# Attention's scores by pairs of heads, in the two halves of TensorE's rows

## The chip, the cores and the metric

The kernel runs on one core of a Trainium2 chip. The time is that of the device, in microseconds, for one execution of the whole program: the median of several runs, and one more execution that the hardware profiler recorded. Engines are called as in the profile: PE is TensorE (matmul; PEld its weight loads), DVE is VectorE, ACT is ScalarE, POOL is GpSimd and SP issues the large DMAs.

## What is computed

The reference is an encoder of two layers on 512 tokens of width 1024, in float32. Each layer mixes tokens in three parallel groups, then applies experts and a gated embedding:

```python
for i in range(DEPTH):                       # 2 layers
    xn = rmsnorm(x, g_mix[i])
    proj = xn @ w_in[i]                      # split into the inputs of the groups
    y_a = gmlp_spatial_gating(...)           # 4 groups x 64
    y_b = dilated_attention(b_q, b_k, b_v, positions, ...)   # 6 heads x 64
    y_c = gated_deltanet(...)                # 6 heads x 64, forward and backward scans
    x = x + concat(y_a, y_b, y_c) @ w_out[i]
    x = x + expert_choice_ffn(rmsnorm(x), ...)               # 16 experts
    x = x + rmsnorm(p[i] @ w_ple[i]) * sigmoid(rmsnorm(x) @ w_ple_gate[i])
```

In `dilated_attention` q and k are normed per head and partly rotated. Three patterns of window and dilation are mixed by their softmax denominators. That equals one softmax over all 512 keys with a mask that holds the logarithm of how many patterns allow a key (and -1e30 where none does), which is how the kernel computes it.

## The kernel before

`mixer` (L363) does the three groups of a layer. It first projects and prepares them; then the scan of the gated delta net, `gdn_scan` (L907), runs as the leading work, and three other pieces of work fill the time in which it waits: attention's v projection (`attn_v`, L595), attention itself (`core`, L608) and the first part of the output projection (`w_out_first`, L1015), one after the other. All four are generators that yield a number after each piece.

`interleave` (L446) sets the order. It runs three pieces of the fill, then again and again one piece of the scan and as many pieces of the fill as the scan's piece asked for: the number that a scan piece yields (`FILLS`, 1.9, 1.5 and 1.1) is added to what is owed, the number that a fill piece yields is its price and is taken off, and the next scan piece comes once 0.5 or less is owed. PE follows the pieces in just this order, since each is issued after the last PE instruction of the piece before (`in_order`, L427). Instructions on the other engines are ordered by a planner that estimates times, each engine working off its own queue in order. What is left of the fill when the scan has ended follows it (L421), then the rest of the delta net (`gdn_out`, L985, which norms and gates the scan's sum and transposes it), and the second part of the output projection (`w_out_last`, L1034).

A step of the scan treats one chunk of 32 tokens in both directions; there are 16. Its pieces on PE are pK (L929), pV (L943), pS (L958) and pO (L969). Between them DVE makes tm (L932) and rr (L936) from pK, ACT copies pV to vn (L947), DVE adds pS to the state St (L962) and adds up the outputs (L977, L979), in the later half with POOL (L980). Each step waits for the state of the last.

In attention a q tile holds two heads, one in partitions 0 to 63 and the other in 64 to 127. `attn_qk` (L464) keeps each q tile twice, with zeros in the other head's half (L473 to L475), so that a matmul over all 128 rows with the k tile of both heads gives the scores of one head. `core` goes over units of one head, one tile of 128 queries: `first` makes the scores (128 x 512) in one PSUM bank out of two, and lets DVE add the mask and take the maximum (L621), ACT take the exponential (L624) and DVE divide by the sum (L626); `second`, two units later, transposes the result by PE (L632) and copies it by ACT (L634); `third`, for each pair of heads, multiplies by v (L641), and `split` stores the result in two parts. The prices are 0.9 for `first`, 0.5 for `second` and 0.9 for `third`. Each float32 matmul shows in the profile as two records, a transpose as one.

Weights of the projections are split into a high and a low half as they come in (`wnext`, L311), by ACT (L330) and POOL (L332, wlo); they lie in slots that are shared with other tensors, and a split can start once such a slot is free.

Of the kernel before, what the change touches and what calls it, by code (L numbers as in the profile page):

```python
# [11 lines left out]
F32 = mybir.dt.float32  # L12
F32R = mybir.dt.float32r
I32 = mybir.dt.int32
AF = mybir.ActivationFunctionType
# [6 lines left out]
S = 512  # L22
DEPTH = 2
NT = S // 128
# [9 lines left out]
THETA = 500000.0  # L34
C_AU, C_BQ, C_CQ, C_GATE, C_A = 0, 512, 1664, 2816, 3200
SLOTS = 12

OWED = 0.5

# [70 lines left out]
class K:  # L110
# [252 lines left out]
    def mixer(self, l):  # L363
        nc, tc, A = self.nc, self.tc, self.A
        with tc.tile_pool(name=f"mix{l}", bufs=1, reuse_waits="tile") as mp:
            self.mp = self.sm = mp
            self.t = lambda i, shape, name: mp.tile(shape, F32, tag=f"t{i}", name=name, bufs=2)
            self.p1 = lambda shape, name: mp.tile(shape, F32, tag="p1", name=name, bufs=3)
            self.p2 = lambda shape, name: mp.tile(shape, F32, tag="p2", name=name, bufs=2)
            self.one = lambda shape, name: mp.tile(shape, F32, tag=name, name=name, bufs=1)  # L370

            for tag, n, bufs in (("qk", 1024, 2), ("amask", S + 384, 1), ("wsT", 512, 1), ("mcst", CROUTE - CKEEP, 1),
                                 ("p1", 512, 3), ("p2", 512, 2)):
                for _ in range(bufs):
                    mp.tile([128, n], F32, tag=tag, name="place", bufs=bufs)
            self.mark("norm")
            g = self.gslot("grow")[:, :D]
            self.row(g, l, "g_mix")
            win, wo = A["w_in"][l], A["w_out"][l]
            specs = [(win[:, c:c + n], n, KD) for c, n in  # L380
                     [(C_AU, 256), (C_AU + 256, 256)]]
            specs += [(win[512 * i:512 * i + 512, C_GATE:C_GATE + 408], 408, 4) for i in range(2)]
            specs += [(win[:, c:c + n], n, KD) for c, n in
                     [(C_CQ + 128 * b[0], 128 * len(b)) for b in QKV_BLOCKS]
                     + [(C_BQ + 256 * i, 256) for i in range(3)]]
            specs += [(win[512 * i:512 * i + 512, C_BQ + 768:C_BQ + 1152], 384, 4) for i in range(2)]
            specs += [(wo[0:640, c:c + n], n, 5) for c, n in WO_COLS]
            specs += [(wo[640:1024, 512 * i:512 * i + 512], 512, 3) for i in range(2)]
            self.wplan(specs)
            wuv = [self.wnext()]  # L390
            if l == 0:
                self.load_x(range(1, NT))
            xs = self.gslot("xs").rearrange("p (t d) -> p t d", t=2)
            tv = lambda name: self.slot(name).rearrange("p (k n) -> p k n", k=4)
            self.xh, self.xl = [tv("xh") for _ in range(2)], [tv("xl") for _ in range(2)]
            for t in range(NT):
                if t == 2:
                    wuv.append(self.wnext(pieces=4))
                self.norm(t, g, xs[:, t % 2, :])
                self.norm_T(t, xs[:, t % 2, :], self.xh, self.xl)  # L400
            self.setup2(l)
            self.gmlp(l, wuv)
            self.gate_decay(l)

            qkv = self.gdn_qkv(l)
            next(qkv)
            self.gdn_chunk(l)
            wq = self.wnext(ahead=False)
            next(qkv, None)
            self.gdn_inv(l)  # L410
            self.gmlp_out(l)
            if l == 0:
                self.trig()
            nc.scalar.dma_start(self.amask, A["amask"])
            self.attn_qk(l, wq)
            self.gdn_inv_T(l)
            wv = [self.wnext(small=True), self.wnext()]

            other = chain(self.attn_v(l, wv), self.core(l), self.w_out_first(l))
            self.interleave(self.gdn_scan(l), other)  # L420
            for _ in other:  # L421
                pass
            self.wo2 = [self.wnext() for _ in range(2)]
            self.gdn_out(l)
        self.w_out_last(l)
# [38 lines left out]
    def attn_qk(self, l, wq):  # L464
        self.mark("attn_qk")
        nc, mp = self.nc, self.mp
        v, act, pe, pool_e = nc.vector, nc.scalar, nc.tensor, nc.gpsimd

        at = [self.slot("att") for _ in range(3)]
        qT = self.qT = [a[:, 0:2 * S].rearrange("p (e n) -> p e n", e=2) for a in at]  # L470
        kT = self.kT = [a[:, 2 * S:3 * S] for a in at]
        self.vat = [a[:, 3 * S:].rearrange("p (t n) -> p t n", t=NT) for a in at]
        for q in qT:  # L473
            pool_e.memset(q[64:128, 0, :], 0.0)
            pool_e.memset(q[0:64, 1, :], 0.0)  # L475

        g2 = self.small([128, 2, 64], "g2")
        o = PR["q_g"][0]
# [6 lines left out]
        gT = self.small([128, 2], "gT")  # L485
# [6 lines left out]
        def second(i, t, qk):  # L492

            pt = self.pc([128, 2, 128], "qkTp")
            for j in range(2):
                pe.transpose(pt[:, j, :], qk[:, t, 2 * j:2 * j + 2, :].rearrange("p h d -> p (h d)"), self.ident)
            ts = slice(t * 128, (t + 1) * 128)
            for j in range(2):
                b = 2 * i + j
                if b < 3:  # L500
                    act.activation(qT[b][0:64, 0, ts], pt[0:64, j], AF.Copy, scale=gT[0:64, 0:1])
                    act.activation(qT[b][64:128, 1, ts], pt[64:128, j], AF.Copy, scale=gT[64:128, 0:1])
                else:
                    act.activation(kT[b - 3][:, ts], pt[:, j], AF.Copy, scale=gT[:, 1:2])

# [100 lines left out]
                self.nc.scalar.activation(self.vat[j][:, t, :], p[:, 128 * j:128 * j + 128], AF.Copy)  # L606

    def core(self, l):  # L608
        nc = self.nc
        v, act, pe = nc.vector, nc.scalar, nc.tensor  # L610
        yb = [self.slot("yTb")[:, :3 * S].rearrange("p (j n) -> p j n", j=3) for _ in range(2)]
        self.yTb = yb
        PTs = {}

        def first(j, t, hp):
            p = self.pb([128, S], "sc")
            pe.matmul(p, self.qT[j][:, hp, t * 128:(t + 1) * 128], self.kT[j], start=True, stop=True)
            P = self.p1([128, S], "P")
            mx = self.small([128, 1], "mx", 3)
            sm_ = self.small([128, 1], "smx", 3)  # L620
            v.tensor_tensor_reduce(P, p, self.amask[:, 384 - 128 * t:384 - 128 * t + S], scale=1.0,  # L621
                                   scalar=-3e38, op0=ALU.add, op1=ALU.max, accum_out=mx)
            v.tensor_scalar(mx, mx, -1.0, None, op0=ALU.mult)
# [19 lines left out]
            ts = slice(t * 128, (t + 1) * 128)  # L643
            self.split(yb[0][:, j, ts], yb[1][:, j, ts], po)

        units = [(j, t, hp) for j in range(3) for t in range(NT) for hp in range(2)]
        Ps = {}
        for i in range(len(units) + 3):
            self.mark("core")
            if i < len(units):  # L650
                Ps[i] = first(*units[i])
                yield 0.9
            if 0 <= i - 2 < len(units):
                self.mark("core")
                second(*units[i - 2], Ps.pop(i - 2))
                yield 0.5
            if i - 3 >= 0 and units[i - 3][2]:
                self.mark("core")
                third(*units[i - 3][:2])
                yield 0.9  # L660


    def gate_decay(self, l):
# [833 lines left out]
```

## Time and profile before

| | |
|---|---|
| median of three runs | 1959.53 us (1959.13 to 1962.07) |
| the profiled execution | 1958.17 us, span 1956.2 us |
| PE busy | 1799.0 us, 92% of the span |
| DVE busy | 930.7 us, 48% |
| ACT busy | 523.6 us, 27% |
| POOL busy | 457.6 us, 23% |
| attention's core in layer 0, first scores to last product with v | 255.87 to 353.00 us |
| the same in layer 1 | 1222.00 to 1319.00 us |

The profiled execution took 1958.17 us as a whole; times in the trace count from the start of its span. Busy times of the engines overlap, so their shares don't add up to one. Matmuls are pipelined: the shown duration of one reaches into the next, and what a row of equal matmuls costs is better read from one start to the next.

### The profile page before, as it was taken

To read this page: it belongs to the slowest core of one execution; us is meant where nothing else is said; L and a number is where in the kernel's file an instruction comes from. 1 tells how busy PE (TensorE), PEld (TensorE's weight loads), DVE (VectorE), ACT (ScalarE), POOL (GpSimd) and SP (SyncE) were. 2 spreads that over 40 slices of the span, in tenths; PEclk is the share of its full clock that TensorE was granted. 3 is DMA by queue.
4 is the path that set the end of the run, shared out by engine and by line. 5 is a ranking of instruction groups with operands and counts; after the bars stand their busy time and mean duration, and the time that the engine had idled before them with its cause. 6 is when DMAs were issued, how large, how long until landed. Compare 5 with 4: busy or idle time off the path is not lost.

```text
span 1956.2 us, 30065 instructions
## 1 busy us (share of the span) xinstructions
PE 1799.0 (92%) x12216; PEld 1126.8 (58%) x12216; DVE 930.7 (48%) x2088; ACT 523.6 (27%) x1213; POOL 457.6 (23%) x402
## 2 busy tenths in 40 slices
PE   5898698979999999999988978899799999999998
PEld 5777665864434444335987767568544343443368
DVE  5879868661211111422788896786511212114135
ACT  4334444231111101102443344452211010011032
POOL 3544413420000003201645352233100000022033
PEclk9989889989999999999998978899799999999999
DMA  5212020287899999999242020204798999999981
GB/s 169 87 34 60 17 85 16 109 321 296 347 412 412 390 412 411 366 414 374 85 131 82 21 71 24 76 2 168 305 356 345 412 406 395 415 372 393 414 289 65
DMA packets 168730, 467.46 MB, mean 239 GB/s; under 512 B 11664, under 2 KB 68496, under 8 KB 168592
## 3 DMA queue, kind: packets, MB, share of 16 engines
q1 hardware_dynamic: 161504, 458.46, 61.0%
q10 hardware_dynamic: 7088, 7.09, 1.2%
q8 instruction: 96, 1.57, 0.3%
q14 instruction: 42, 0.34, 0.1%
HBM read 461.32 MB, written 4.19 MB: 238 GB/s over the span
## 4 chain that ended last, share of the span: by engine, by line
PE 68%; DVE 21%; ACT 4%; issue 3%; POOL 2%; DMA 2%; SPq 1%; ACTq 0%; DVEq 0%; POOLq 0%
PE pGt L1270 15%; PE pUp L1270 11%; PE pY L1270 10%; DVE acc L770 3%; PE xep L1198 2%; DVE rr L936 2%; PE ysc L1289 2%; PE xep L1199 2%; PE op L340 1%; PE ysc L1290 1%; PE pV L943 1%; PE plep L1164 1%; PE pgp L342 1%; PE pgp L340 1%; PE pY L1385 1%
## 5 line engine op out<-in xcount | busy, mean ns | idle before, releaser
L1270 PE MATMUL pUp<-w,xe 128*64 128x512 f32 x800 | 200.8, 595 | 0.0
L1270 PE MATMUL pGt<-w,xe 128*64 128x512 f32 x640 | 200.4, 600 | 0.0
L332 POOL TENSOR_TENSOR wlo<-w,whi 128x512 fp32r<-128x512 f32 (+5 forms) x66 | 161.3, 2463 | 114.7 <-ACT whi L330 99.9
L1270 PE MATMUL pY<-w,hidT 128*64 128x512 f32 x720 | 186.9, 596 | 0.0
L1337 POOL TENSOR_TENSOR x<-x,hh 128x1024 f32<-128x1024 f32 x8 | 18.9, 2358 | 615.5 <-DVE x L1295 615.4
L1270 PEld LDWEIGHTS pUp<-w,xe 128*64 128x64 f32 x800 | 70.7, 137 | 101.8 <-issue 98.0
L1295 DVE TENSOR_TENSOR x<-ysc,x 128x512 f32<-128x512 f32 x96 | 63.2, 686 | 117.9 <-PE ysc L1290 117.9
L1270 PEld LDWEIGHTS pGt<-w,xe 128*64 128x64 f32 x640 | 58.6, 136 | 99.7 <-issue 97.6
L1270 PEld LDWEIGHTS pY<-w,hidT 128*64 128x64 f32 x720 | 64.1, 136 | 89.9 <-issue 87.4
L1270 PE MATMUL pGt<-wx,xe 128*64 128x512 f32 x320 | 114.4, 603 | 0.3
L1328 DVE SCALAR_TENSOR_TENSOR hid<-sg,gsl,pUp 128x512 f32<-128x512 f32 x32 | 23.7, 747 | 159.7 <-PE pUp L1270 158.1
L1354 DVE SCALAR_TENSOR_TENSOR yl<-pY,gsl,yh 128x512 fp32r<-128x512 f32 x28 | 21.0, 751 | 165.2 <-ACT yh L1353 163.7
L1321 DVE SCALAR_TENSOR_TENSOR sg<-sg,pGt 128x512 f32<-128x512 f32 x32 | 21.8, 686 | 132.2 <-ACT sg L1320 132.2
L330 ACT ACTIVATE whi<-w 128x512 fp32r<-128x512 f32 (+5 forms) x66 | 68.0, 1058 | 38.5 <-PE op L341 15.8
L342 PE MATMUL pgp<-whi,gTl 128*128 128x256 f32 x256 | 72.8, 292 | 3.9 <-DVE gTl L271 3.9
L329 POOL TENSOR_TENSOR w<-w,pp 128x512 f32<-128x512 f32 x32 | 32.4, 1047 | 179.2 <-DMA w<-in_w_ple_gate_dram 107.7
L1320 ACT ACTIVATE sg<-pGt,gsl 128x512 f32<-128x512 f32 x32 | 21.8, 687 | 192.2 <-PE pGt L1270 190.2
L340 PE MATMUL pgp<-whi,gTh 128*128 128x256 f32 x256 | 73.0, 289 | 0.0
L1200 ACT ACTIVATE xe<-xep,pp 128x256 f32<-128x256 f32 x64 | 30.2, 474 | 158.7 <-PE xep L1199 158.7
L341 PE MATMUL pgp<-wlo,gTh 128*128 128x256 f32 x256 | 72.4, 288 | 0.0
L1198 PE MATMUL xep<-OH,hh 128*128 128x256 f32 x256 | 69.1, 304 | 2.5 <-DVE OH L1186 2.5
L1344 ACT ACTIVATE hidT<-htp 128x512 f32<-128x512 f32 x32 | 19.1, 597 | 193.5 <-PE htp L1343 193.5
(404 smaller groups left out, 4277.0 us busy)
## 6 DMA issues: line engine op xcount, KB each, us to landing
w<-in_w_e_up_dram SPq DMA_DIRECT2D x100, 1024.0 KB, 14.6
w<-in_w_e_down_dram SPq DMA_DIRECT2D x90, 1024.0 KB, 11.3
w<-in_w_e_gate_dram SPq DMA_DIRECT2D x80, 1024.0 KB, 12.9
wx<-in_w_e_gate_dram SPq DMA_DIRECT2D x40, 1024.0 KB, 11.6
wx<-in_w_e_up_dram SPq DMA_DIRECT2D x28, 1024.0 KB, 12.2
wx<-in_w_e_down_dram SPq DMA_DIRECT2D x22, 1024.0 KB, 8.3
wd<-in_w_e_down_dram SPq DMA_DIRECT2D x32, 512.0 KB, 8.8
w<-in_w_in_dram SPq DMA_DIRECT2D x14, 1024.0 KB, 5.0
```

The lines of the kernel that those rows point to most:

```text
L330: self.nc.scalar.activation(rr_(hi[:, ks, :]), wk, AF.Copy)
L332: e.tensor_tensor(rr_(lo[:, ks, :]), wk, hi[:, ks, :], op=ALU.subtract)
L340: pe.matmul(p, lh, rh, start=first, stop=False)
L341: pe.matmul(p, lh, rl, start=False, stop=False)
L342: pe.matmul(p, ll, rh, start=False, stop=last)
L770: v.scalar_tensor_tensor(acc, raw[:, kk:kk + S], conv[:, b, kk:kk + 1], acc, op0=ALU.mult, op1=ALU.add)
L936: v.tensor_tensor(rr[kl[dr], :], vtok[kl[dr], tl, :], fl(tm[kl[dr]]), op=ALU.subtract)
L1198: pe.matmul(p, rr_(hh[:, t, ks]), OHf[:, t, :], start=(t == 0), stop=False)
L1199: pe.matmul(p, rr_(hl[:, t, ks]), OHf[:, t, :], start=False, stop=(t == NT - 1))
L1270: pe.matmul(pt[nh][64 * ei:64 * ei + 64, :], lhs[:, kk, 64 * ei:64 * ei + 64], wt[ei][k][:, nh * 512:nh * 512 + 512], start=(kk == 0), sto ...
L1289: pe.matmul(p, rr_(OT[:, t, :]), rr_(yh[:, ns]), start=True, stop=False)
L1295: v.tensor_tensor(xv, p, xv, op=ALU.add)
```

## The change

The zeros and the second copy of q go. q and k tiles now hold two heads each in the two halves of the partitions, and a pair of heads is one unit. Its scores are four matmuls over 64 rows, in turns for the upper and the lower half of the array's rows, each for half of the keys; the two heads write to the two PSUM banks. The softmax of both heads follows. The order within a step of `core` becomes scores of unit i, product with v of unit i - 2, transposes of unit i - 1; the prices are 1.1, 0.9 and twice 0.5. The p1 buffers, which hold the exponentials, become four, and the DMA scratch is set to 256.

```diff
+P1 = 4
...
-            self.p1 = lambda shape, name: mp.tile(shape, F32, tag="p1", name=name, bufs=3)
+            self.p1 = lambda shape, name: mp.tile(shape, F32, tag="p1", name=name, bufs=P1)
...
-        qT = self.qT = [a[:, 0:2 * S].rearrange("p (e n) -> p e n", e=2) for a in at]
-        kT = self.kT = [a[:, 2 * S:3 * S] for a in at]
-        self.vat = [a[:, 3 * S:].rearrange("p (t n) -> p t n", t=NT) for a in at]
-        for q in qT:
-            pool_e.memset(q[64:128, 0, :], 0.0)
-            pool_e.memset(q[0:64, 1, :], 0.0)
+        qT = self.qT = [a[:, 0:S] for a in at]
+        kT = self.kT = [a[:, S:2 * S] for a in at]
+        self.vat = [a[:, 2 * S:3 * S].rearrange("p (t n) -> p t n", t=NT) for a in at]
...
-                    act.activation(qT[b][0:64, 0, ts], pt[0:64, j], AF.Copy, scale=gT[0:64, 0:1])
-                    act.activation(qT[b][64:128, 1, ts], pt[64:128, j], AF.Copy, scale=gT[64:128, 0:1])
+                    act.activation(qT[b][:, ts], pt[:, j], AF.Copy, scale=gT[:, 0:1])
...
-        def first(j, t, hp):
-            p = self.pb([128, S], "sc")
-            pe.matmul(p, self.qT[j][:, hp, t * 128:(t + 1) * 128], self.kT[j], start=True, stop=True)
-            P = self.p1([128, S], "P")
-            mx = self.small([128, 1], "mx", 3)
-            sm_ = self.small([128, 1], "smx", 3)
+        def first(j, t):
+
+            ps = [self.pb([128, S], "sc") for _ in range(2)]
+            for half in range(2):
+                cs = slice(half * S // 2, (half + 1) * S // 2)
+                for hp, p in enumerate(ps):
+                    hl = slice(64 * hp, 64 * hp + 64)
+                    pe.matmul(p[:, cs], self.qT[j][hl, t * 128:(t + 1) * 128], self.kT[j][hl, cs], start=True, stop=True)
+            return [softmax(p, t) for p in ps]
+
+        def softmax(p, t):
+            P = mp.tile([128, S], F32, tag="p1", name="P", bufs=P1)
+            mx = self.small([128, 1], "mx", 4)
+            sm_ = self.small([128, 1], "smx", 4)
...
-        units = [(j, t, hp) for j in range(3) for t in range(NT) for hp in range(2)]
+        units = [(j, t) for j in range(3) for t in range(NT)]
         Ps = {}
-        for i in range(len(units) + 3):
+        for i in range(len(units) + 2):
             self.mark("core")
             if i < len(units):
                 Ps[i] = first(*units[i])
+                yield 1.1
+            if 0 <= i - 2:
+                self.mark("core")
+                third(*units[i - 2])
                 yield 0.9
-            if 0 <= i - 2 < len(units):
-                self.mark("core")
-                second(*units[i - 2], Ps.pop(i - 2))
-                yield 0.5
-            if i - 3 >= 0 and units[i - 3][2]:
-                self.mark("core")
-                third(*units[i - 3][:2])
-                yield 0.9
+            if 0 <= i - 1 < len(units):
+                for hp in range(2):
+                    self.mark("core")
+                    second(*units[i - 1], hp, Ps[i - 1][hp])
+                    yield 0.5
...
-    nc = bacc.Bacc("TRN2", target_bir_lowering=False, num_devices=1)
+    nc = bacc.Bacc("TRN2", target_bir_lowering=False, num_devices=1, dynamic_dma_scratch_size=256)
```

## Rows read from the trace of the kernel before

**Rows 1.** The page, the chain that ended last: shares of the span by engine

```profile
PE 68%; DVE 21%; ACT 4%; issue 3%; POOL 2%; DMA 2%; SPq 1%; ACTq 0%; DVEq 0%; POOLq 0%
```

**Rows 2.** Windows by stage: length, busy us of PE, PEld, DVE, ACT, POOL, then PEclk, DMA

```profile
255.87:353.00 97.13, 85.47 (x1275) 57.74 (x1273) 75.39 (x210) 48.50 (x106) 27.46 (x22) 0.91 0.11 41
375.50:392.50 17.00, 15.40 (x109) 15.13 (x105) 13.45 (x33) 3.41 (x5) 5.87 (x5) 1.00 0.67 263
392.50:416.00 23.50, 23.18 (x129) 19.17 (x128) 15.16 (x51) 7.83 (x16) 0.80 (x2) 1.00 0.68 245
1222.00:1319.00 97.00, 85.31 (x1278) 57.60 (x1273) 75.27 (x210) 48.50 (x106) 27.43 (x22) 0.91 0.12 42
```

**Rows 3.** Windows by scan step: three undisturbed steps, one of three heads, two stalled

```profile
307.12:332.20 25.08, 23.78 (x396) 16.29 (x395) 20.14 (x64) 13.73 (x31) 6.41 (x7) 1.00 0.01 2
260.30:269.68 9.38, 8.61 (x131) 5.62 (x131) 7.83 (x26) 6.21 (x13) 0.50 (x2) 1.00 0.39 139
269.68:285.32 15.64, 12.06 (x130) 8.48 (x129) 10.34 (x23) 4.58 (x10) 5.42 (x3) 0.67 0.00 1
293.10:307.12 14.02, 10.07 (x130) 6.74 (x129) 10.90 (x23) 4.42 (x11) 4.79 (x2) 0.76 0.16 48
```

**Rows 4.** Timeline of PE, from a scan step: start, us, what (xcount are records)

```profile
321.89 0.86 PE L969 MATMUL pO<-vn,QKm 32*32 32x64 f32 x24
322.68 1.12 PE L617 MATMUL sc<-att 128*128 128x512 f32 x2
323.74 0.58 PE L929 MATMUL pK<-St,KQT 64*64 64x64 f32 x24
324.25 0.66 PE L632 MATMUL ptp<-cst,P 128*128 128x128 f32 x4
324.74 1.02 PE L617 MATMUL sc<-att 128*128 128x512 f32 x2
```

**Rows 5.** Timeline of PE in the experts: two column halves

```profile
485.33 0.59 PE L1270 MATMUL pY<-w,hidT 128*64 128x512 f32 x1
485.34 0.59 PE L1270 MATMUL pY<-wx,hidT 128*64 128x512 f32 x1
```

**Rows 6.** Groups of DVE in 307.12:332.20: count, then busy us and mean ns

```profile
L621 DVE CUSTOM_DVE_ANT_0 P<-sc,amask 128x512 f32<-128x512 f32 x7 | 4.7, 686 | 1.3 <-PE sc L617 1.3
L626 DVE TENSOR_SCALAR P<-P,smx 128x512 f32<-128x512 f32 x7 | 3.7, 522 | 0.1
L625 DVE RECIPROCAL smx<-smx 128x1 f32<-128x1 f32 x7 | 1.1, 162 | 2.9 <-ACT P L624 2.8
```

**Rows 7.** Timeline of POOL: a weight's low half

```profile
270.38 4.24 POOL L332 TENSOR_TENSOR wlo<-w,whi 128x1920 fp32r<-128x1920 f32 x1 [0.35 <-ACT whi L330]
```

**Rows 8.** Timeline of DVE: the scan's subtraction; a w_out addition and two steps of gdn_out

```profile
271.74 3.87 DVE L936 TENSOR_TENSOR rr<-vtok,tm 32x384 f32<-32x384 f32 x2
...
383.63 0.56 DVE L1031 TENSOR_TENSOR x<-op,x 128x384 f32<-128x384 f32 x1 [0.43 <-PE op L342]
...
385.76 2.88 DVE L182 SCALAR_TENSOR_TENSOR ro__4169<-nr,ro__4169 128x24 f32<-128x24 f32 x1
...
389.12 0.18 DVE L182 SCALAR_TENSOR_TENSOR ro__4169<-nr,ro__4169 128x24 f32<-128x24 f32 x1
```

**Rows 9.** Timeline of PE: after the stall; last scan matmuls; first transposes of gdn_out

```profile
275.18 1.97 PE L943 MATMUL pV<-rr,XT 32*32 32x64 f32 x24 [3.48 <-DVE rr L936]
...
374.71 0.86 PE L969 MATMUL pO<-vn,QKm 32*32 32x64 f32 x24
...
392.54 0.93 PE L1010 MATMUL ycp<-cst,o_sum 128*128 128x128 f32 x6
```

**Rows 10.** Windows: the stretches of lower clock behind the two stalls

```profile
275.10:285.30 10.20, 10.02 (x98) 7.35 (x98) 5.00 (x14) 2.54 (x6) 0.83 (x1) 0.51 0.01 2
300.50:305.00 4.50, 4.49 (x36) 2.81 (x38) 1.69 (x7) 2.14 (x5) 0.00 (x0) 0.50 0.50 149
```

**Rows 11.** Timeline of POOL: the first of the six memsets of q's padding

```profile
174.99 0.52 POOL L474 MEMSET att<- 64x512 f32 x1
```

More of the change, by code (lines that the diff above doesn't have):

```diff
@@ L372, in mixer @@
             for tag, n, bufs in (("qk", 1024, 2), ("amask", S + 384, 1), ("wsT", 512, 1), ("mcst", CROUTE - CKEEP, 1),
-                                 ("p1", 512, 3), ("p2", 512, 2)):
+                                 ("p1", 512, P1), ("p2", 512, 2)):
                 for _ in range(bufs):
@@ L608, in core @@
     def core(self, l):
-        nc = self.nc
+        nc, mp = self.nc, self.mp
         v, act, pe = nc.vector, nc.scalar, nc.tensor
```

## The prediction

> **What bounds the kernel now.** I read the page's chain first [rows 1]: 68% of the end is TensorE (PE), 21% VectorE (DVE). The change touches one stage of each layer, so I then cut the span into windows by stage [rows 2]. Attention's core runs beside the delta-net scan for 97.1 us in layer 0 and 97.0 us in layer 1, with the same busy times in both, so one layer is worked out and doubled. PE is busy 85.5 of the 97.1, but at a granted clock of 0.91; DVE 75.4. Steps of the scan [rows 3] show why: three undisturbed ones take 25.08 us (8.36 each) with PE busy 23.78, so PE is the bound and DVE, 20.14, is close behind. Two steps are far longer, 15.64 and 14.02. In the first, POOL works on a weight's low half for 4.24 us [rows 7], DVE's two rr subtractions take 3.87 [rows 8], and pV starts after 3.48 us of idle PE [rows 9]; behind each such wait PE runs at 0.50 to 0.51, half its 2.4 GHz, for 10.2 and 4.5 us [rows 10]. The two steps together lie 12.9 us over two of 8.36.
>
> What sets the scan's pace is a price list, not a time: a whole scan step releases 1.9 + 1.5 + 1.1 = 4.5 units of fill. The 97.1 us held 44.4 units of core, so 9.87 steps, and without the 12.9 a step took (97.13 - 12.94) / 9.87 = 8.53 us.
>
> **The scores.** One piece of scores (two records) starts 1.06 us before the next when it follows a scan piece; after transposes its 1.02 ends within the next piece, by some 0.1 as neighbours do, so about 0.9 [rows 4]. Mean 0.98, a pair of heads 1.96. Afterwards a pair is eight records of half the columns, and each half of the array's rows streams what one head streamed. If the halves run side by side the pair costs 0.98, if not 1.96. The nearest row is of column halves: two records of the experts start 0.01 us apart and both take 0.59 [rows 5]; and pK, 24 records over row and column halves, passes in 0.51 [rows 4]. I take 0.98: 12 pairs x 0.98 = 11.8 us less PE work a layer.
>
> The Trainium skill says otherwise on one point: its page "TensorEngine Tiling (Array Packing)", section "Key Properties", states that changing the tiling mode drains the engine. The pieces of rows 4 differ by 0.1 to 0.2 us after a change of shape, so the rule shows here; charged once more to each pair it would turn the sum below from -1.6 to +0.8 us a layer, which is the third rival.
>
> **Where the saving appears.** By the prices a pair falls from 2 x 0.9 + 2 x 0.5 + 0.9 = 3.7 units to 1.1 + 0.9 + 1.0 = 3.0; twelve pairs give 8.4 units less. The scan's own pieces are unchanged, so its steps keep asking for 4.5 units, and w_out's first part moves up by 8.4 units. In the scan's part PE therefore loses 11.8 us and gets 8.4 units of w_out: the fill's prices add up to 16 for v, 44.4 for core and 25.7 for w_out, 86.1, of which the three first pieces and the scan's 16 steps (2.6 + 15 x 4.5) spend 73.1; the other 13.0 made the tail with 15.4 us of PE [rows 2], 1.18 each, so 8.4 are 9.9 us. The scan ends about 1.9 us earlier, not 11.8. This needs core steps of 8.3 us (eight of them are left, and eight times 8.53 - 8.3 is 1.8, which I use).
>
> Does DVE allow 8.3? It has 20.14 / 3 = 6.7 us a step with 7/3 heads [rows 3, 6]. A step will hold 1.5 pairs, three heads. A head is 0.69 and 0.52 for the two large operations and about 0.3 for two small ones [rows 6], 1.5; so 6.7 + 0.67 x 1.5 = 7.7 us, 93% of 8.3. The one step of before with three heads had DVE 7.83 and took 9.38, but PE was busy 8.61 of that [rows 3]; taking away 1.5 pairs x 0.98 leaves 7.9. So a core step lies between 7.9 and 9.4; at 8.53 the scan ends when it did. Bounds a layer: 8 x (7.9 - 8.53) = -5.0 and 8 x (9.38 - 8.53) = +6.8. I take 8.3, -1.8.
>
> **The tail.** From the last scan matmuls (374.71, 0.79 long) to gdn_out's first transposes (392.54) are 17.0 us [rows 9], filled with w_out. Afterwards w_out has 15.4 - 9.9 = 5.5 us left, and PE then waits for gdn_out's chain on POOL, ACT and DVE, which also starts at the scan's end. That chain ran in the 17.0 us with 2.7 us of stall in one operation (2.88 where the same later takes 0.18 [rows 8]) and with w_out's additions between its steps (0.56, the same rows); without the stall and four or five of them it needs 12, with the stall 15. I take 13.5, so 3.5 us are gained (2 to 5) and PE idles 13.5 - 5.5 = 8 us.
>
> That idle is longer than the 3.48 us behind which the clock fell to a half. The next stage is PE's (23.18 busy of 23.50 at clock 1.00 [rows 2]), so a lower clock costs there half its length: 2.25 us by the shorter stretch, 5.1 by the longer [rows 10]. I take the mean, 3.7. Were the gap closed, 0.
>
> **The rest**, nothing each. The six memsets (0.52 each [rows 11], 3.1 a layer) leave POOL ahead of weight halves that take their time from DVE whether early or late; bounds -3.1 and 0. One eviction by ACT in place of two per transposed q tile lies beside DVE's triangular inverse, whose end opens the scan; bounds, by the memsets' size, the same. A fourth p1 buffer holds the second pair, as the third held the third head; what waits for it is the score's reduction. third now stands before second; behind its transposes' copy on ACT wait the scan's vn copies, as before. The new wait is that a pair needs both score banks free; they are freed by two reductions (0.69 each) at least 1.9 units earlier, so it is covered unless DVE falls behind. The earlier users of p1 find one buffer more, and the smaller DMA scratch issues nothing.
>
> **Sum.** A layer: -1.8 - 3.5 + 3.7 = -1.6; two layers -3.2. From the profiled execution's own 1958.17 (span 1956.2) that is 1955.0; the median of the runs is 1.36 above it, so 1956.3 us.
>
> **Rivals.** (1) *DVE takes over the core steps.* Both heads' reductions, 1.4 us together, arrive in one burst ahead of the scan's tm and rr, and pV waits. At 9.1 us a step: 8 x 0.57 = +4.6, with the tail's +0.2 +4.8 a layer, +9.6: 1969. It decides from 8.53 on. For it: DVE was 83% of its three-head step; against: PE was the longer there. In a sentence of its own: the Trainium skill, same page, section "PSUM Bottleneck", says that tiling speeds TensorE and not the emptying of PSUM, and DVE's near 80% of a step agrees. (2) *The halves don't run side by side*: the pair costs 1.96 at a price of 1.1, w_out's 9.9 come on top, +10.1 a layer: 1980. Against it stand rows 5 and pK. (3) *The change of shape eats the gain*: 0.2 us more for each of 12 pairs, +0.8 a layer: 1961, no change. For it, the 1.06 against 0.9; against, that the score piece paid it already after a scan piece. (4) *One of the two long steps goes.* The weight halves of rows 7 land at another place of the step; if one misses rr, 12.9 / 2 = 6.5 less a layer: 1956.3 - 13 = 1943. For it, that two out of two hit rr; against, that DVE has fewer gaps.
>
> **Chances.** Forecast 0.42 (1949 to 1960), rival 1 0.22, rival 2 0.05, rival 3 0.16, rival 4 0.15. This kernel's measurement tells 0.2%, 3.9 us, from no change. Faster: about half of the forecast's case and rival 4, 0.37. Same: the other half and most of rival 3, 0.33. Slower: rivals 1 and 2 and the rest of 3, 0.30. The range runs to 1942 (rival 4) and to 1972 (both layers near the step of 9.38); rival 2 and two vanished long steps lie outside. Without the others the forecast's own range is 1949 to 1960.
>
> **What would show it.** Right: scores' records in two banks starting together, a pair passing in about 1 us; core steps near 8.3; w_out starting some two steps earlier; PE idle for about 8 us before gdn_out's first transposes with a clock near 0.5 behind. Wrong: a pair of 1.5 or more; steps over 8.6 with pV waiting for rr behind the reductions; gdn_out's transposes less than 12 us after the last scan matmuls; other long steps than two a layer.

## The result, and the profile after

The change made the kernel slower: the median is 1996.9 us against 1960.8 us of the kernel before on the same chip. The ratio on record, which is not the quotient of these two medians (1.018), is 1.0157 (95% interval 1.013 to 1.0184). The forecast was 1956.3 us, with 1942 to 1972 as its range. The profiled execution took 2001.78 us (span 2000.0), 43.8 us of span more than before; it is the slowest of four, which go from 1987.6 to 2001.8.

The page after, the chain that ended last (answers to [rows 1]): the shares hardly move, so they don't tell where the time went.

```profile
PE 70%; DVE 20%; ACT 4%; issue 2%; DMA 2%; POOL 1%; ACTq 0%; SPq 0%; DVEq 0%; POOLq 0%
```

Windows by stage do. First the kernel before, the whole scan (first pK to the last pO) of layers 0 and 1; then the kernel after: the same two, and of layer 0 the tail up to gdn_out's transposes and the stretch from there to the experts' first gather (xep), which answers to the tail and what follows it in [rows 2]. Columns: window, length, busy us of PE, PEld, DVE, ACT and POOL, then the granted clock, DMA share and GB/s.

```profile
234.20:375.50 141.30, 128.00 (x1897) 94.07 (x1896) 96.08 (x259) 59.26 (x135) 40.89 (x32) 0.94 0.12 41
1200.90:1341.60 140.70, 128.07 (x1896) 94.14 (x1895) 94.42 (x253) 59.21 (x135) 40.49 (x31) 0.94 0.12 41
```

```profile
235.30:402.10 166.80, 147.31 (x1998) 118.74 (x1997) 95.93 (x256) 61.72 (x136) 40.27 (x32) 0.81 0.17 62
1227.10:1386.00 158.90, 135.95 (x1998) 109.76 (x1997) 94.00 (x256) 60.98 (x136) 40.29 (x32) 0.88 0.18 64
402.10:417.00 14.90, 6.38 (x55) 6.19 (x52) 10.11 (x32) 1.92 (x4) 5.59 (x5) 0.85 0.00 0
417.00:464.00 47.00, 33.38 (x189) 28.71 (x189) 30.91 (x109) 16.19 (x32) 10.05 (x6) 0.79 0.81 310
```

The scan grew by 25.5 us in layer 0 and by 18.2 in layer 1. The tail shrank by 2.1 and 2.2 us, the stretch behind it grew by 1.9 and 1.2 (45.1 and 45.3 us before), and the scan began 1.1 us later in layer 0. These add up to 43.6 of the 43.8 us.

Three numbers can be read from such a row. Idle of PE is the length less PE's busy time: 13.3 us before, 19.5 after in layer 0. What the lower clock costs is (1 - clock) x length, since in a stretch at half clock half of the time is lost: 8.5 before, 31.7 after. The rest of the busy time is PE's work at full clock: 119.5 before, 115.6 after (it fell by less than the scores saved, because w_out moved up into the scan). So the scores' saving is there, and twice as much went into the clock. These three numbers are used for every kernel below. They are rough: idle time that falls into a stretch at half clock counts both as idle and as clock loss, 1.2 us a layer before, 1.9 after, and 3.4 at most (po_g_p18).

The scores themselves did what was forecast. PE's timeline after, a pair at full clock, answers to [rows 4]: eight records, and 1.07 us later comes pK (before, a pair took 1.96).

```profile
331.89 1.14 PE L620 MATMUL sc<-att 64*128 64x256 f32 x8
332.96 0.29 PE L936 MATMUL pK<-St,KQT 64*64 64x64 f32 x4
```

What PE waited for beside layer 0's core is in the waits, first of the kernel before, then after (engine, line, releaser: us, times, longest):

```profile
PE pV L943 <- DVE rr L936: 10.5, 11, 4.0
```

```profile
PE ptp L638 <- DVE yTb L273: 13.7, 7, 4.1
...
PE pK L936 <- DVE St L969: 2.7, 2, 2.3
...
PE pV L950 <- DVE rr L943: 0.4, 2, 0.2
```

Seven times, for 13.7 us (and seven times, for 16.1 us, in layer 1), the transposes (ptp) wait for VectorE's last operation on another tile, the product with v (L273 in `split` subtracts ACT's rounded copy from po). The reason is PSUM: ptp and po share two banks (`pc`). In the new order of a step come po, the first head's transposes, the second head's transposes; these take the third turn and so the bank of po, which is free only after ACT's copy and DVE's subtraction. One such wait in full, timeline after:

```profile
295.03 1.84 PE L647 MATMUL po<-PT,att 128*64 128x128 f32 x16
...
297.02 4.24 POOL L334 TENSOR_TENSOR wlo<-w,whi 128x1920 fp32r<-128x1920 f32 x1 [5.98 <-ACT P L630]
297.10 4.43 DVE L632 TENSOR_SCALAR P<-P,smx 128x512 f32<-128x512 f32 x1
...
301.64 0.49 DVE L632 TENSOR_SCALAR P<-P,smx 128x512 f32<-128x512 f32 x1
302.05 0.28 DVE L273 TENSOR_TENSOR yTb<-po,yTb 128x128 fp32r<-128x128 f32 x1
302.39 1.12 PE L638 MATMUL ptp<-cst,P 128*128 128x128 f32 x4 [4.14 <-DVE yTb L273]
```

The short subtraction stands on DVE's queue behind the softmax of the pair, and there one operation of 0.49 us takes 4.43 beside POOL's low half of a weight (such a one hit rr in [rows 7, 8]). PE idles 4.14 us and runs its next 1.12 us of transposes at half clock (0.66 for the same at full clock in [rows 4]).

### The profile page after: what moved, and what is told of

Same layout as the page of the kernel before. It is cut to its first block, busy times and chain, and to the rows that moved or that the text cites. A ratio compares the mean times of both kernels' runs of the same rounds, so it can differ in the third digit from the quotient of the medians.

```text
span 2000.0 us, 30199 instructions
## 1 busy us (share of the span) xinstructions
PE 1816.0 (91%) x12312; PEld 1154.8 (58%) x12312; DVE 920.6 (46%) x2088; ACT 513.5 (26%) x1189; POOL 453.5 (23%) x390
## 4 chain that ended last, share of the span: by engine, by line
PE 70%; DVE 20%; ACT 4%; issue 2%; DMA 2%; POOL 1%; ACTq 0%; SPq 0%; DVEq 0%; POOLq 0%
PE pGt L1277 14%; PE pUp L1277 11%; PE pY L1277 10%; DVE acc L777 3%; PE xep L1205 2%; PE ysc L1296 2%; PE op L342 2%; PE xep L1206 2%; PE sc L620 2%; PE ysc L1297 1%; PE op L343 1%; PE op L344 1%; PE plep L1171 1%; PE pO L976 1%; PE pgp L344 1%
## 5 line engine op out<-in xcount | busy, mean ns | idle before, releaser
L332 ACT ACTIVATE whi<-w 128x512 fp32r<-128x512 f32 (+5 forms) x66 | 68.1, 1057 | 40.7 <-PE op L343 13.3
L777 DVE SCALAR_TENSOR_TENSOR acc<-raw,pp,acc 128x512 f32<-128x512 f32 x72 | 63.9, 887 | 15.8 <-ACT acc L775 13.0
## 6 DMA issues: line engine op xcount, KB each, us to landing
wx<-in_w_e_gate_dram SPq DMA_DIRECT2D x40, 1024.0 KB, 11.8
wx<-in_w_e_up_dram SPq DMA_DIRECT2D x28, 1024.0 KB, 12.2
```

Of the source, the lines that this page charges most:

```text
L332: self.nc.scalar.activation(rr_(hi[:, ks, :]), wk, AF.Copy)
L777: v.scalar_tensor_tensor(acc, raw[:, kk:kk + S], conv[:, b, kk:kk + 1], acc, op0=ALU.mult, op1=ALU.add)
```

## The experiments

Theories, as the expectations name them. W: the wait for po's bank is the cause, by idle and the half clock behind it. D: VectorE is the bound (the prediction's first rival). P: matmuls over half the rows keep the clock down by themselves. R1: the cheaper price is what costs; R2: a step is set by the chain over VectorE and ScalarE, whatever PE saves. C: PE's saved time comes back as idle and half clock. B: issuing the pair at once makes a burst for VectorE. Scan, idle, clock loss and work are means of the two layers, in us, worked out as above from the profiled execution; the ratio is to the kernel before on the same chip. Each row's scan is one execution, and the runs of one kernel spread (po_g took 1968.7 to 1981.8 us), so a difference of 2 us a layer is weak by itself.

| kernel | ratio (95% interval) | scan | idle | clock loss | work |
|---|---|---|---|---|---|
| before | 1 | 141.0 | 13.0 | 8.5 | 119.6 |
| after | 1.0157 (1.013 to 1.0184) | 162.9 | 21.2 | 25.4 | 116.2 |
| po_g | 1.0061 (1.0039 to 1.0083) | 149.2 | 13.6 | 17.9 | 117.7 |
| padded_pair | 1.0128 (1.0102 to 1.0154) | 155.5 | 15.0 | 13.2 | 127.3 |
| padded_pair_po_g | 1.0022 (1.0002 to 1.0043) | 147.2 | 7.9 | 10.3 | 129.0 |
| packed_old_p2_3 | 1.0021 (1.0005 to 1.0038) | 149.1 | 15.9 | 14.2 | 119.0 |
| old_p2_3_p18 | 1.0027 (0.9998 to 1.0056) | 147.7 | 18.2 | 20.7 | 108.8 |
| pair_old_padded | 0.9987 (0.9971 to 1.0004) | 143.1 | 11.2 | 12.2 | 119.7 |
| twice_old | 1.0118 (1.0072 to 1.0165) | 156.8 | 22.7 | 15.7 | 118.4 |
| warm_old | 1.0038 (1.0019 to 1.0057) | 150.5 | 17.0 | 15.8 | 117.6 |
| before_act_mult | 0.9923 (0.99 to 0.9946) | 136.5 | 10.6 | 6.2 | 119.8 |
| act_mult | 0.9965 (0.9946 to 0.9983) | 143.2 | 11.5 | 10.7 | 121.0 |

The work column bears the account out: the three kernels with scores over all rows at before's prices lie at 119.6 to 119.8, the packed one at those prices at 108.8, and 7 to 12 us more stand in the scan where the cheaper price pulls w_out out of the tail.

**Is it the bank? (po_g, padded_pair)** In po_g the product with v takes one of the scan's four banks:

```diff
-            po = self.pc([128, 128], "po")
+            po = self.pg([128, 128], "po")
```

> The changed kernel, but the product with v goes to one of the scan's four PSUM banks instead of one of the two that the transposes use. Theory W (the new order makes the second head's transposes wait for the bank of the product with v, which DVE's subtraction L273 frees; PE idles 1 to 4 us about ten times a layer and its clock falls to a half): no transposes wait for yTb any more, clock in the core above 0.9, core steps back from 11.9 to about 8.5 us, time 1945 to 1965. Theory D (DVE is the bound of the core steps with 1.5 pairs each): steps stay over 10 us, 1985 or more. Theory P (matmuls over half of the rows keep the clock at a half by themselves): scores stay at 2.0 us a pair and the clock near 0.65, 1985 or more.

Measured 1975.6 us. None of the transposes waits for yTb any more, and the scan is 13.7 us a layer shorter. The time lies between what W and what D and P expected: W holds for the larger part, and 0.6% stay.

padded_pair is the changed kernel with q padded as before (the lines for q's tiles are left out here), so that a pair's scores cost 1.96 us again:

```diff
...
-                    hl = slice(64 * hp, 64 * hp + 64)
-                    pe.matmul(p[:, cs], self.qT[j][hl, t * 128:(t + 1) * 128], self.kT[j][hl, cs], start=True, stop=True)
+                pe.matmul(p, self.qT[j][:, hp, t * 128:(t + 1) * 128], self.kT[j], start=True, stop=True)
```

> The changed kernel's pair units, order, prices and four p1 buffers, but the scores from q padded with zeros over all 128 rows, as before the change. W: the waits for yTb stay, and the scores cost 0.9 us a pair more on top: 1990 to 2025. P: with no half-row matmuls the clock is back near 1.0 in the core, 1960 to 1980. D: steps about as long as in the changed kernel, 1985 to 2005.

Measured 1987.2 us, in D's range and just under W's: the order with its prices makes most of the loss, without any half rows, so P is not the main cause. Both edits together:

> q padded as before, the order and prices by pairs as in the changed kernel, but po from the scan's banks: what the order costs once the bank wait is gone, without packing. If the bank wait was the order's whole cost (W alone): 1960 to 1970 us, like before. If bursts of two reductions and the cheaper price cost by themselves (R1, or VectorE bound): 1972 to 1990 us.

Measured 1969.3 us, 1.0022. So the bank costs 1.0% in this order, with packed scores (1.0157 to 1.0061) and with padded ones (1.0128 to 1.0022). That is shown twice, by intervals that lie apart. Of the loss of 1.57% there remain 0.4% by packing in this order (1.0022 to 1.0061) and 0.2% by the order and the prices without the bank (1.0022, hardly clear of 1).

**Before's order with packed scores (packed_old_p2_3), and the buffers alone (before_p1_4).** In the first, a pair's scores come in one piece at 1.1, but `second` and `third` stand as before, with three PT buffers; the second is the kernel before with a fourth p1 buffer and the smaller DMA scratch.

```diff
...
-            if i < len(units):
-                Ps[i] = first(*units[i])
-                yield 0.9
+            if i < len(units) and i % 2 == 0:
+                Ps[i], Ps[i + 1] = first(*units[i][:2])
+                yield 1.1
...
```

> The scores by pairs in the halves of the rows, but second and third in the order of before (transposes of head 0, product with v of the pair before, transposes of head 1), the same prices, and a third buffer for the transposed exponentials. W: no transposes wait for yTb, core steps near 8.5 us, 1945 to 1965. D: steps over 10 us, 1985 or more, since DVE has as much to do in a step. P: clock near 0.65 in the core, 1985 or more.

> The kernel before with only the fourth p1 buffer and the small DMA scratch of the change. All theories: no change, 1956 to 1966; if it moved by more, a part of the 36 us would be the buffers' and not the order's.

Measured 1968.8 us (1.0021) and 1960.7 us (0.9994, 0.9977 to 1.0012). The fourth p1 buffer and the scratch cost nothing. The order of before mends most of the loss too (1.0157 to 1.0021, just above W's range), but 11 us of PE's work a layer bring no gain.

**The prices (old_p2_3_p18, po_g_p18, price18, p85).** `yield 1.1` becomes `yield 1.8` in packed_old_p2_3, po_g and the changed kernel, so that a pair asks for 3.7 units as before; p85 keeps 1.1 and raises `second` from 0.5 to 0.85.

> Packed scores in the order of before (third behind second, three PT buffers), a pair at 3.7 units as before. R1: 1940 to 1957 us, pK-to-pK in the core under 8.3 us, tail full. R2: 1958 to 1970 us, steps as before or longer with PE idle in them, DVE or ACT ending the waits.

> po from the scan's banks (no bank wait) and a pair's score piece at price 1.8 instead of 1.1, so that a pair asks for 3.7 units as before. Theory R1 (the cheaper price is what eats the rest: it puts 1.5 pairs of reductions into a step and empties the tail): steps fall below 8.5 us, PE in the tail is busy about 15 of 17 us again, no half clock after it: 1945 to 1960 us. Theory R2 (a step is set by the chain over VectorE and ScalarE whatever PE saves): PE only gains idle time and half clock, 1962 to 1978 us, no faster than before.

> The changed kernel with nothing but the price 1.8. Bank wait stays in each pair, with fewer pairs in a step: W says the waits of ptp for yTb stay near 25 a layer and the time lies between 1975 and 1995 us; if the price alone were the cause (R1 without W) it falls to 1945 to 1962 us.

> packed_old_p2_3 with the price of second (transposes) 0.85 instead of 0.5: a pair asks for 3.7 units as before, but the scores keep 1.1, so that 1.9 units hold as much PE work as before. If the prices' fit to PE's time decides (theory C): fewer waits of pV for rr than old_p2_3_p18's 16 us a layer and of ptp for PT than packed_old_p2_3's 9, full tail: 1940 to 1958 us. If a step is bound otherwise (D): 1960 to 1970 us.

Measured 1966.4 us (1.0027), 1989.3 (1.0114, 1.0068 to 1.016), 1983.8 (1.0094, 1.0066 to 1.0121) and 1985.1 (1.0094, 1.0078 to 1.011). R1 falls: the dearer price fills the tail again (17.0 us, and 45.0 behind it as before), and still none is faster than before. The first lies where R2 expected it. price18 has W's time but not its reason: PE's waits for yTb fall to 2.8 us in both layers together (29.8 in the changed kernel), and idle grows all the same (22.7 us a layer). po_g_p18 and p85 came out above everything expected, with 23.0 and 22.0 us of idle. In price18 and po_g_p18, with the score's piece dear and short, the wait is another one, pV for rr: 13.2 us in price18 and 16.9 in po_g_p18 beside layer 0's core, where the changed kernel has 0.4.

**Where the packed scores' saving goes (pair_old_padded against old_p2_3_p18).** pair_old_padded is the kernel before with both heads' scores issued together, column halves in turn, at price 1.8, with the buffers of packed_old_p2_3: old_p2_3_p18 with all the rows of the array.

```diff
...
+            for half in range(2):
+                cs = slice(half * S // 2, (half + 1) * S // 2)
+                for hp, p in enumerate(ps):
+                    pe.matmul(p[:, cs], self.qT[j][:, hp, t * 128:(t + 1) * 128], self.kT[j][:, cs], start=True, stop=True)
...
```

> The kernel before (q padded, all rows of the array) with nothing but this: both heads' scores are issued together, their column halves in turn as packed, and both reductions behind them, at price 1.8; one P buffer and one PT buffer more. Theory B (burst: issuing the pair together makes VectorE first wait and then take two reductions ahead of the scan's tm and rr): 1975 to 1995 us, like twice_old (1987), scan about 152 to 158 us. Rival P (half rows of the array are what costs): 1958 to 1968 us, like before.

Measured 1961.9 us, 0.9987: B falls, issuing the pair at once costs nothing. The time lies where rival P, as it is put here (half rows are what cost), expected it. The scans of pair_old_padded and of old_p2_3_p18, layers 0 and 1, columns as above:

```profile
233.40:375.60 142.20, 130.09 (x1944) 106.01 (x1943) 91.62 (x259) 58.62 (x135) 41.03 (x32) 0.93 0.12 41
1201.40:1345.50 144.10, 133.72 (x1944) 108.46 (x1943) 89.30 (x253) 58.70 (x135) 40.55 (x31) 0.90 0.12 40
```

```profile
234.90:382.30 147.40, 129.41 (x1945) 103.94 (x1944) 91.66 (x253) 59.93 (x135) 40.63 (x31) 0.86 0.11 39
1202.40:1350.40 148.00, 129.54 (x1944) 103.57 (x1943) 91.27 (x253) 59.29 (x135) 40.39 (x31) 0.86 0.12 39
```

PE is busy about as long, but at a clock of 0.86. Packing alone (with the copies of q that belong to it), a layer: 10.9 us less work, 7.0 more idle, 8.5 more clock loss, so 4.6 us longer; the ratios lie 0.4% apart, and their intervals just overlap. The two other pairs that differ by packing point the same way: padded_pair_po_g to po_g -11.3, +5.7, +7.6 (2.0 longer), padded_pair to the changed kernel -11.1, +6.2, +12.2 (7.3 longer), though these two intervals overlap more. What is shown is that packing gains nothing here; that it costs 0.3 to 0.4% rests on three differences of like sign. How idle turns into clock loss stands in old_p2_3_p18's windows:

```profile
261.00:263.00 2.00, 0.66 (x4) 0.42 (x4) 1.90 (x6) 0.25 (x1) 0.00 (x0) 1.00 1.05 377
263.00:265.00 2.00, 0.00 (x0) 0.00 (x0) 1.84 (x9) 2.00 (x6) 0.00 (x0) 0.65 0.36 125
265.00:267.00 2.00, 1.02 (x14) 0.82 (x16) 1.28 (x3) 0.33 (x1) 0.00 (x0) 0.50 0.00 0
267.00:277.00 10.00, 10.00 (x119) 7.77 (x114) 5.39 (x18) 4.72 (x9) 0.94 (x1) 0.50 0.01 2
277.00:279.00 2.00, 2.00 (x34) 1.40 (x32) 1.64 (x4) 0.93 (x2) 1.51 (x1) 0.94 0.00 0
```

By the timeline, PE stands still ahead of pV for 3.36 us:

```profile
265.87 0.39 PE L949 MATMUL pV<-rr,XT 32*32 32x64 f32 x2 [3.36 <-DVE rr L942]
```

The clock falls from 2.4 to 1.2 GHz, and it stays there while PE is busy for ten us without a gap.

**Half rows, or idle? (twice_old, warm_old)** twice_old issues each pair's packed scores twice, so PE's work is that of before; warm_old adds one matmul 128x384, its result overwritten, ahead of each pV beside the core.

```diff
...
-            for half in range(2):
+            for half in (0, 1, 0, 1):
...
```

> old_p2_3_p18 with each pair's scores issued twice (the second overwrites the first with the same values): half-row matmuls as packed, PE's time for a pair about 2.1 us as before the change, order and prices as before. Theory C (idle of PE is what drops the clock; the saved time comes back as idle and half clock): scan 141 to 144 us at a clock near 0.94 again, 1955 to 1965 us, no slower than old_p2_3_p18 with half its scores. Rival P (matmuls on half the rows themselves keep the clock down): clock stays near 0.86, scan 155 us or more, 1975 to 2000 us.

> old_p2_3_p18 and, in the steps beside attention's core, one matmul 128x384 of constants more (about 0.9 us, its result is overwritten) ahead of pV, where PE waits for rr. Theory C (packing's saved PE time comes back as idle ahead of pV and as half clock behind it): the waits for rr vanish, fewer half-clock stretches, and although about 10 us of PE work are added in each layer the time is no more than 1966, likely 1945 to 1962 us. Rival (PE time counts as such, the half clock costs little): about 10 us a layer more, 1975 to 1990 us.

Measured 1987.4 us (1.0118) and 1973.7 us (1.0038). Neither came out clean. warm_old: 8.8 us of work more, 1.2 less idle and 4.9 less clock loss, so 2.8 us longer a layer; the added work is paid back by two thirds, not in full. twice_old speaks against C as I had put it: its work is that of pair_old_padded, 118.4 against 119.7, yet it idles 22.7 us against 11.2. Its time and its scan (156.8 us) lie where P had them. P's mechanism is not what the trace shows, since the clock rose to 0.90 and most of the loss is idle; but that packed scores cost something by another way than PE's time for them is what this run says, and which way it does not say.

The traces show one thing that old_p2_3_p18 and twice_old share and pair_old_padded doesn't have: another order on VectorE. Timeline of DVE in old_p2_3_p18, the first pair's softmax and the state's two additions (St), then the same in pair_old_padded:

```profile
258.28 0.34 DVE L968 TENSOR_TENSOR St<-St,pS 128x192 f32<-128x192 f32 x1
258.54 0.15 DVE L629 TENSOR_SCALAR mx<-mx 128x1 f32<-128x1 f32 x1
259.25 0.16 DVE L631 RECIPROCAL smx<-smx 128x1 f32<-128x1 f32 x1 [0.56 <-ACT P L630]
259.32 0.33 DVE L968 TENSOR_TENSOR St<-St,pS 128x192 f32<-128x192 f32 x1
```

```profile
258.07 0.34 DVE L968 TENSOR_TENSOR St<-St,pS 128x192 f32<-128x192 f32 x1
258.33 0.15 DVE L629 TENSOR_SCALAR mx<-mx 128x1 f32<-128x1 f32 x1
258.39 0.34 DVE L968 TENSOR_TENSOR St<-St,pS 128x192 f32<-128x192 f32 x1
```

In the packed kernel the second St stands behind a reciprocal that waits for ScalarE's exponential, and pK of the next step waits for St. From the end of a step's pS to the end of its St I read, as means over the ten steps of each layer's core, 0.91 and 0.75 us in pair_old_padded, 1.69 and 1.54 in old_p2_3_p18, 1.57 and 1.80 in twice_old. But PE seldom waits for it. The waits of PE in layer 0's scan, old_p2_3_p18 and then pair_old_padded:

```profile
PE pV L949 <- DVE rr L942: 11.9, 15, 3.4
PE pK L935 <- DVE St L968: 3.3, 3, 2.1
PE pS L964 <- ACT vn L953: 1.5, 2, 1.0
```

```profile
PE pV L949 <- DVE rr L942: 9.2, 17, 2.1
PE pS L964 <- ACT vn L953: 1.1, 2, 0.6
...
PE pK L935 <- DVE St L968: 0.4, 1, 0.4
```

With layer 1 (11.9, 2.8 and 2.5 us against 8.8, 0.3 and 0.6), the 7.0 us of idle that packing adds are 2.7 ahead of pK for St, 2.9 ahead of pV for rr and 1.2 ahead of pS for vn, as means. So the place of St stands directly behind less than half of them. That the changed order on VectorE is the cause is argued, not shown: no run changed it alone.

**VectorE (act_mult, before_act_mult, po_g_act, act_p18).** P times 1/sum goes from VectorE to ScalarE, in packed_old_p2_3, before, po_g and old_p2_3_p18.

```diff
-            v.tensor_scalar(P, P, sm_, None, op0=ALU.mult)
+            act.activation(P, P, AF.Copy, scale=sm_[:, 0:1])
```

> packed_old_p2_3 (1968.8) with P times 1/sum on ScalarE in place of VectorE (24 x 0.49 us a layer leave VectorE). Theory D (VectorE sets the core's steps): steps get about 0.7 us shorter, 1945 to 1960 us. Theory C: the chain over ScalarE (exp, this, PT, vn) gets longer, no gain, 1962 to 1980 us.

> The kernel before with the same move to ScalarE, as the control of act_mult. If VectorE's waits (rr) cost before its clock: 1945 to 1957 us; if ScalarE's chain takes its place: 1958 to 1975 us. By theory D it gains less than act_mult does against packed_old_p2_3, since PE bounds it.

> The changed kernel with its two repairs: po from the scan's banks, P times 1/sum on ScalarE. Expected from po_g (1975.6) less what the move gave in the two other orders (0.6 to 0.8%, 11 to 15 us): 1958 to 1966 us. Theory D says more, under 1950 us, since here bursts of two reductions meet rr.

> Packed scores in the order of before, 3.7 units a pair, P times 1/sum on ScalarE. Compared with before_act_mult (0.9923) it differs by packing alone. Theory C: PE's saved 11 us a layer come back as idle and half clock once more: 1950 to 1965 us, not below before_act_mult's 1951. Theory D (with VectorE relieved PE's saving shows): 1930 to 1945 us.

Measured 1959.1 us (0.9965), 1951.3 (0.9923), 1964.6 (0.9995, 0.9975 to 1.0016) and 1965.7 (1.0012, 0.9992 to 1.0032). The move brings 0.6 to 0.8% in three of the four, and their times lie in the ranges expected; before_act_mult is the fastest kernel of the study, without packing. D had expected less there than in act_mult; by the ratios it is more (0.8% against 0.6%), but the intervals don't part them. act_p18 came out just above what C expected and far from D's 1930 to 1945 us. It differs from before_act_mult not by packing alone, as its expectation says, but by the pair's piece and the buffers too. The move doesn't make the packing pay: with it, the packed kernels stay 0.4% or more above before_act_mult.

Why the move gains is only in part shown. The scans of before_act_mult, layers 0 and 1, columns as above:

```profile
239.70:372.60 132.90, 125.01 (x1897) 92.88 (x1896) 81.62 (x229) 74.40 (x159) 39.91 (x31) 0.96 0.13 44
1197.90:1338.10 140.20, 126.96 (x1896) 93.72 (x1895) 87.45 (x234) 74.35 (x159) 41.02 (x32) 0.95 0.12 41
```

Layer 0 is 8.4 us shorter than before and layer 1 only 0.5, though 11.8 us leave VectorE in both. In layer 0 one of the two long steps is gone (14.0 us before, 7.5 now): there the weight's low half, at 301.41, starts when the second rr (from 301.19) is under way and does not hold it, where in layer 1 and in the kernel before rr starts within the low half and takes more than 4 us. So in this execution most of the gain is the prediction's fourth rival, a low half that misses rr. Whether VectorE's relief made it miss, or chance did, no run tells.

**The second head's softmax one piece later (split_softmax, split_act).** Only the first head's reduction is issued with the pair, the other's ahead of the next `second`; split_act has the move to ScalarE as well.

```diff
...
+            if i < len(units) and i % 2:
+                Ps[i] = softmax(ps[1], units[i][1])
             if 0 <= i - 2 < len(units):
...
```

> Packed scores in the order of before, but only the first head's reduction and exponential are issued with the pair; the second head's come one piece of fill later, as in the kernel before. A pair asks for 3.7 units (1.1, 1.2, 0.5, 0.9). Theory B: the burst is gone and PE's saving shows at last: 1940 to 1957 us. Theory C (the saved time comes back as idle and half clock wherever the reductions stand): 1960 to 1970 us, as old_p2_3_p18.

> split_softmax with P times 1/sum on ScalarE. Theory B: under before_act_mult's 1951, 1930 to 1948 us. Theory C: 1952 to 1965 us.

Measured 1993.4 us (1.0148, 1.0119 to 1.0177) and 1990.9 (1.014, 1.0109 to 1.0171), worse than every expectation. The scans take 157.0 and 160.7 us in split_softmax, with 18.9 and 25.2 idle and a clock of 0.80 and 0.84. Spreading the softmax does not help; what makes it this bad I did not take further.

## Why the prediction was wrong

**The step that failed** is "The rest, nothing each": "third now stands before second; behind its transposes' copy on ACT wait the scan's vn copies, as before. The new wait is that a pair needs both score banks free". I looked for the new wait at the scores' two banks and not at the two that po and ptp share. There the exchanged order makes the second head's transposes wait for a subtraction at the end of DVE's queue. It was put at 0 and is worth 1.0% of the time; in the profiled executions that is 8.3 us a layer of scan with padded and 13.7 with packed scores.

**The scan's sum failed with it, in its form.** "PE loses 11.8 and gets 8.4 units of w_out", so the scan ends 1.8 us earlier: the loss of work measured 10.9 to 11.3, near the forecast. But the sum held idle and clock as they were (core steps 8.53 to 8.3 us). The steps became 13.6 us (pK from 263.68 to 358.93 in seven steps of layer 0, not 11.9, as the expectation of po_g has it), and without the bank, in po_g, 11.3. There each step holds 1.5 pairs in place of 1.2, but at before's prices too packing adds as much idle and half clock as it takes away, and more.

**Right in the mechanism:** the halves run side by side (rival 2 falls). w_out moves up, and PE then idles ahead of gdn_out, forecast 8 us, measured:

```profile
417.01 1.51 PE L1017 MATMUL ycp<-cst,o_sum 128*128 128x128 f32 x6 [8.53 <-DVE o_sum L1014]
```

The same six records took 0.93 in [rows 9], so the half clock behind the idle came as well. Its size: 1.9 and 1.2 us by the stretch to xep, 3.7 forecast. The tail gave 2.1 us, not 3.5: the chain over POOL, ACT and DVE takes 15 us in every kernel with the cheap price, the upper end that the prediction named. The two cancel. From memsets and q's copies no gain shows, as costed: the scan of layer 0 began 1.1 us later.

**Rivals.** The time lies above that of every rival (1980 at most). The first (VectorE takes over, pV waits for rr) is not what the changed kernel shows, 0.4 us of PE's waits in layer 0's core. Where the price is 1.8, though, pV does wait for rr as it says, and the wait for the bank ends on VectorE's queue too. The Trainium skill, page "TensorEngine Tiling (Array Packing)", section "PSUM Bottleneck", says that tiling speeds TensorE and not what empties PSUM. The runs fit it loosely: 11 us less of TensorE's work a layer brought nothing and a move of 11.8 us off VectorE did, but what was moved does not empty PSUM itself; it stands on one queue with what does. The third (change of shape) does not show at its price: at full clock the pair passes in 1.07 us, 0.09 over the forecast and not 0.2. The fourth came true in part: of the two low halves beside the core, one now meets nothing that it holds up, and the other hits the softmax's multiplication (4.43 us in layer 0, 2.51 in layer 1) where both had hit rr. Its gain was lost in the longer steps.

**Still open** is why a packed pair makes PE idle more when nothing but the rows differ, and why twice_old with before's work is 1.3% slower than pair_old_padded. The place of St on DVE's queue fits in part; a run that fixes that order alone would tell. The low halves fall differently too: they hold one multiplication of the softmax for 2.1 and 2.4 us in old_p2_3_p18 (layers 0 and 1) and for 1.4 and 0.9 in pair_old_padded, and in twice_old they hold an rr for 4.05 in layer 0. No run held that fixed either.

## What to carry to other kernels

When the order of the work on an engine is exchanged, list the turns of every rotating buffer, not only of those that the new code names, and see what the last reader of each one stands behind. Work taken out of an engine that covers another's chain need not be time saved: read idle and clock loss of that stretch first, and ask what the chain allows. Here half of the scores' time on PE brought nothing, and a multiplication moved from the second busiest engine of the stage to the third brought 15 us (0.0077 x 1960), part of which may be chance in where a weight's low half fell: look for such a single event before a gain is put down to the relief of an engine.

## What the runs showed of the hardware

Two 64-row fp32 matmul streams in the two halves of the array's rows run side by side: a pair of 128x512 scores takes 1.07 us from its start to the next piece's, and 1.93 with all rows and the same column halves, timeline of PE in pair_old_padded:

```profile
255.17 1.99 PE L620 MATMUL sc<-att 128*128 128x256 f32 x8
257.10 0.74 PE L964 MATMUL pS<-vn,kdec 32*64 32x64 f32 x24
```

The clock at 1.2 GHz outlasts the idle behind which it fell by much: 3.36 us of idle ahead of pV were followed by ten us at half clock with PE busy throughout. And VectorE's multiplication of 0.49 us takes up to 4.43 while POOL works on a weight's low half for 4.24. Not all of VectorE's work is held up. In the kernel before, beside the low half from 270.38 to 274.62 [rows 7], the reduction of the scores and the two tm keep their length, and only rr is held [rows 8]:

```profile
270.42 0.69 DVE L621 CUSTOM_DVE_ANT_0 P<-sc,amask 128x512 f32<-128x512 f32 x1
...
271.04 0.62 DVE L932 TENSOR_TENSOR tm<-pK,ex 128x192 f32<-128x192 f32 x2
```

Those that keep their length read PSUM (sc, pK; beside other low halves pS, pO and po as well, at 0.35, 0.56 and 0.29 us); rr and the softmax's multiplication, which are held until the low half ends if they start within it, read SBUF alone. Operations of 128x1, which read SBUF too, keep their 0.15 us. In act_mult and po_g_act, where ScalarE does the multiplication, the low halves met rr at most in their last 0.8 us (1.24 us in act_mult), and no operation of VectorE in these scans took over 1.4, while in before_act_mult they hit rr as before, once in layer 0 and twice in layer 1.
